# Two transformer-like blocks on one core: the first block's branch products between the gate chunks

## The chip, the core and the metric

The kernel runs on one core of a Trainium2 chip. Its engines are PE (matrix products), DVE (elementwise on vectors), ACT (activations and casts), POOL and SP, which issues most of the loads. Time is the device time of one execution in microseconds (us); the median of several executions is compared.

## What is computed

A sequence of 256 positions with 1024 channels goes through a first block and then twice through a second one. The change touches the first part of the first block, which in the reference is

```
u = rms_norm(h, norm_mix_pre)
proj = u @ w_in            # 10 slots of 256 columns, then 4 x 1024 gate columns
y_a = rg_lru_branch(a_x, a_gate, ...)        # linear recurrence   (branch 0)
y_b = pool_branch(p_x, ...)                  # window means        (branch 1)
y_c = hgrn2_branch(c_q, c_f, c_i, c_g, ...)  # chunked recurrence  (branch 2)
y_d = short_conv_branch(s_b, s_c, s_x, ...)  # 3-tap convolution   (branch 3)
merged = sum over k of sigmoid(gate_logits[k]) * (y[k] @ w_branch[k])
h = h + rms_norm(merged @ w_out, norm_mix_post)
```

## The kernel before, in words

Channels lie on partitions and the 256 positions on the free axis. Every weight is used in float32 precision by splitting it: a chunk of 128x2048 words is loaded by SP into `raw` (2 buffers), ACT casts it to `hi` (L190, 3 buffers) and DVE subtracts to get `lo` (L192, 3 buffers). A chunk then feeds 48 matmuls (L230), three for each pair of a weight tile and an input tile: hi x H, hi x L and lo x H, where H and L are the split input. `weights` takes chunks from a queue that `plan1` writes down in order of use, and calls for two chunks beyond the one it hands out.

A result of a chunk goes to a PSUM tile `mm` of 128x512. PSUM is parted by the pools of `Builder`: three tiles for `mm`, one for sums, three for the small products of the branches, one for later use.

The order of the first block's program is: the ten slot chunks (`win` 0 to 9), then the branches `hgrn`, `short_conv`, `pool`, `lru`, then sixteen gate chunks, four each for the branches 3, 1, 0, 2 (`BORDER`), then the four branch products in the same order, then `wout` (`post`). A gate chunk's result is multiplied by the norm (L946, DVE) and put through a sigmoid (L947, ACT). A branch product uses one `wbr` chunk for four PSUM tiles of 12 matmuls; each tile is multiplied by its gate (L958, DVE) and, from the second branch on, added to the merged result M (L961, DVE). With the last branch M is split into H and L in permuted order (L346 on ACT, L347 on DVE), which are the input `xs` of `wout`.

`lru` is the linear recurrence. On DVE it has a convolution (L1069 to L1073), two reciprocals of 128x512 (L1088, L1091), a chain of multiplications (L1092 to L1097), two scans (L1100) and the last product (L1108), which `finish` splits.

Nothing of the order on an engine is written by hand. Engines take their instructions in an order that is fixed when the program is built: where several could start next on an engine, by the builder's own estimate of times, the one that stands first in the program is taken; an instruction from further on is put in where those before it must still wait. Each engine then follows its own list strictly, and waits where an operand is late.

Of the kernel before, what the change touches and what calls it, by code (L numbers as in the profile page):

```python
# [17 lines left out]
P = 128  # L18
NT = 256
# [738 lines left out]

WINDOWS = (2, 4, 8, 16)
MLEV = (1, 2, 4, 8, 16)  # L760
BORDER = (3, 1, 0, 2)


def layout1(A):
# [24 lines left out]
    m = [s == t]  # L789
    for h in MLEV:  # L790
        m.append((s // (2 * h) == t // (2 * h)) & (s % (2 * h) < h) & (t % (2 * h) >= h))
# [10 lines left out]

class Block1(Builder):
    def plan1(self):
        for j in SLOTS + [10 + 4 * k + j for k in BORDER for j in range(4)]:
            self.plan("win", j)
        for k in BORDER:
            self.plan("wbr", k)
        self.plan_pairs("wout", 4, KD)
        self.plan_pairs("wup", 16, KD)  # L810
        self.plan_pairs("wdown", 4, DFF // P)
# [59 lines left out]
    def block1(self):  # L871
        nc = self.nc
        v = nc.vector

        X = self.X
        XS = [self.slot(8 + j, [P, 2, NT]) for j in range(4)]
        self.X = XS
        norm = self.Norm(self, "norm_mix_pre")

        def first(j):  # L880
            nc.sync.dma_start(XS[j], self.d["xs"][:, 2 * j:2 * j + 2])
            norm.feed(j, False)

        self.ahead = 0
        self.weights("win", SLOTS[0], first=first)
        nc.scalar.dma_start(self.ident, self.d["ident"])
        H, L = norm.H, norm.L
        pt0 = self.mm("win", SLOTS[0], KD, H, L)
        norm.sums()
        norm.done()  # L890
        self.X = X
        nc.sync.dma_start(self.prmt[:, self.n1:], self.d["prm"][:, self.n1:])
        bd = self.slot(16, [P, 6, P])
        nc.sync.dma_start(bd.rearrange("p a b -> p (a b)"), self.d["bd"])
        lm = self.slot(7, [P, 6, P], I32)
        nc.sync.dma_start(lm.rearrange("p a b -> p (a b)"), self.d["lmask"])
        s6 = self.slot(6, [P, 4, NT])
        winv = self.half(s6, 0)
        nc.sync.dma_start(winv, self.d["winv"].rearrange("p (a b) -> p a b", a=2))
        bones = self.tp.tile([P, 2], F32, name="bones", tag="bones", bufs=1)  # L900
        nc.sync.dma_start(bones, self.d["bones"])
        for j in range(4):
            nc.sync.dma_start(X[j], self.d["xp"][:, 2 * j:2 * j + 2])

        sp = self.softplus_neg(self.prm("lru_lambda"))
        c4 = self.tp.tile([P, 2], F32, name="c4", tag="c4", bufs=1)
        v.tensor_scalar(c4, sp, 4.0, None, op0=ALU.mult)
        hb = self.tp.tile([P, 4], F32, name="hba", tag="hba", bufs=1)
        v.tensor_scalar(hb[:, :2], self.prm("lru_b_a"), 0.5, None, op0=ALU.mult)
        v.tensor_scalar(hb[:, 2:], self.prm("lru_b_x"), 0.5, None, op0=ALU.mult)  # L910
        lb = self.tp.tile([P, 2, 4], F32, name="lb", tag="lbt", bufs=1)
        d = self.prm("hgrn_lower_bound")
        v.tensor_sub(lb[:, :, 0], d, d)
        nc.scalar.activation(lb[:, :, 0], lb[:, :, 0], AF.Exp)
        v.reciprocal(lb[:, :, 1], lb[:, :, 0])
        v.tensor_mul(lb[:, :, 0], lb[:, :, 0], lb[:, :, 1])
        v.tensor_sub(lb[:, :, 2], lb[:, :, 0], lb[:, :, 0])
        v.tensor_scalar(lb[:, :, 3], lb[:, :, 2], -1.0, 1.0, op0=ALU.mult, op1=ALU.add)

        S = [self.slot(i, [P, 4, NT]) for i in range(6)]  # L920
        dest = {0: self.half(S[0], 0), 1: self.half(S[0], 1), 3: self.half(S[2], 0),
                4: self.half(S[2], 1), 5: self.half(S[3], 0), 6: self.half(S[3], 1), 7: self.half(S[4], 0),
                8: self.half(S[4], 1), 9: self.half(S[5], 0)}
        pad = self.slot(1, [P, 2, 16 + NT])
        nc.gpsimd.memset(pad[:, :, :16], 0.0)
        dest[2] = pad[:, :, 16:]
        for j in SLOTS:
            pt = pt0 if j == SLOTS[0] else self.mm("win", j, KD, H, L)
            v.tensor_mul(dest[j], pt, norm.rb2)
        YS = {}  # L930
        self.hgrn(dest, lb, lm, bones, YS)
        self.short_conv(dest, YS)
        self.pool(pad, winv, bd, YS)
        self.lru(dest, bd, c4, hb, S, s6, YS)
        gates = {}
        for n, k in enumerate(BORDER):
            for j in range(4):
                i = n * 4 + j
                if i % 2 == 0:
                    gs = self.slot(8 + i // 2, [P, 4, NT])  # L940
                gates[k, j] = self.half(gs, i % 2)
        M = [gates[BORDER[0], j] for j in range(4)]
        for k, j in gates:
            pt = self.mm("win", 10 + 4 * k + j, KD, H, L)
            g = gates[k, j]
            v.tensor_mul(g, pt, norm.rb2)  # L946
            nc.scalar.activation(g, g, AF.Sigmoid)  # L947
        for k in BORDER:
            h, lo = self.weights("wbr", k)
            YH, YL = YS[k]  # L950
            if k == BORDER[3]:
                MH, ML = self.new_xs()
            for j in range(4):
                pt = self.p_mm.tile([P, 2, NT], F32, name="mm")
                c = slice(j * 512, (j + 1) * 512)
                self.mm_pair(pt, h[:, c], lo[:, c], YH, YL, range(2), True, True)
                g = gates[k, j]
                v.tensor_mul(g, pt, g)  # L958
                if k == BORDER[0]:
                    continue  # L960
                v.tensor_add(M[j], M[j], g)  # L961
                if k == BORDER[3]:
                    for i in range(2):
                        self.split(M[j][:, i].rearrange("p (i a c) -> p c a i", i=16, a=4, c=4),
                                   MH[2 * j + i].rearrange("p (c a i) -> p c a i", c=4, a=4, i=16),
                                   ML[2 * j + i].rearrange("p (c a i) -> p c a i", c=4, a=4, i=16))
        nx = self.Norm(self, "norm_mlp_pre")
        self.post("wout", KD, MH, ML, "norm_mix_post", nx)
        hid = [self.slot(j, [P, 4, NT], F32R) for j in range(16)]
        HH = [hid[k // 2][:, k % 2] for k in range(32)]  # L970
        HL = [hid[k // 2][:, 2 + k % 2] for k in range(32)]
        for j, pt in self.mms("wup", 16, nx.H, nx.L, True):
            if j == 0:
                nx.done(True)
            z = self.t2("z")
            v.tensor_mul(z, pt, nx.rb2)
            f = self.t2("f")
            v.scalar_tensor_tensor(f, z, 0.0, z, op0=ALU.max, op1=ALU.mult)
            self.split(f, hid[j][:, :2], hid[j][:, 2:])
        norm = self.Norm(self, "ffn1_norm0")  # L980
        self.post("wdown", 32, HH, HL, "norm_mlp_post", norm)
        return norm
# [128 lines left out]
    def hgrn(self, dest, lb, lm, bones, YS):  # L1111
# [25 lines left out]
        def products(qs, ks, lev):  # L1137
            ps = [bank() for _ in range(2)]
            for b in range(2):
                bs = slice(b * P, (b + 1) * P)  # L1140
                for i in range(2):
                    for e in range(2):
                        nc.tensor.matmul(ps[e][:, b, i], ks[rows[e], i, bs], qs[rows[e], i, bs], start=True, stop=True)
            for e in range(2):
                v.copy_predicated(sc[e].rearrange("p a b c -> p (a b) c"),
                                  lm[:, lev][:, None, :].to_broadcast([P, 4, P]),
                                  ps[e].rearrange("p a b c -> p (a b) c"))
# [4 lines left out]
        while h <= 128:  # L1152
            qh, kh = self.t2("qh"), self.t2("kh")
            view = lambda t: flat(t).rearrange("p (n two h) -> p n two h", two=2, h=h)
            if h <= 16:
                v.tensor_mul(qh, q, pre)
                v.tensor_mul(kh, k, suf)
                products(qh, kh, 1 + MLEV.index(h))
            else:
# [59 lines left out]
SLOTS = [4, 3, 5, 6, 7, 8, 9, 2, 0, 1]  # L1219
# [44 lines left out]
```

## Time and profile before

| | us |
|---|---|
| median of 3 runs | 1833.76 |
| lowest and highest of them | 1829.9, 1835.49 |
| the profiled execution | 1830.46 |
| its span in the trace | 1828.4 |

The page gives each engine's busy time as a share of the span; times in all views count from the span's start. The block that the change touches takes roughly the first 320 us; the moved code lies between 75 and 222 us.

### The profile page before, as it was taken

To read this page: it belongs to the slowest core of one execution; us is meant where nothing else is said; L and a number is where in the kernel's file an instruction comes from. 1 tells how busy PE (TensorE), PEld (TensorE's weight loads), DVE (VectorE), ACT (ScalarE), POOL (GpSimd) and SP (SyncE) were. 2 spreads that over 40 slices of the span, in tenths; PEclk is the share of its full clock that TensorE was granted. 3 is DMA by queue.
4 is the path that set the end of the run, shared out by engine and by line. 5 is a ranking of instruction groups with operands and counts; after the bars stand their busy time and mean duration, and the time that the engine had idled before them with its cause. 6 is when DMAs were issued, how large, how long until landed. Compare 5 with 4: busy or idle time off the path is not lost.

```text
span 1828.4 us, 32906 instructions
## 1 busy us (share of the span) xinstructions
PE 1764.5 (97%) x14048; PEld 1688.6 (92%) x14048; DVE 1325.3 (72%) x2021; ACT 922.0 (50%) x1047; POOL 46.0 (3%) x69
## 2 busy tenths in 40 slices
PE   7999999999999999989999999999998989999998
PEld 7989899999999987778999999999997778999997
DVE  7886877546765698988876656765598988776653
ACT  5354454435444455467654445444455566654442
POOL 0000000000100000000000000100000000000000
PEclk9999999999999999999999999999999999999999
DMA  7526445554555579886455555555569887355552
GB/s 267 184 93 209 163 160 185 185 185 161 194 185 180 190 220 260 267 227 160 150 187 193 186 170 199 191 188 176 194 202 279 251 234 180 126 198 185 185 185 93
DMA packets 53569, 348.46 MB, mean 191 GB/s; under 512 B 6192, under 2 KB 6320, under 8 KB 14256
## 3 DMA queue, kind: packets, MB, share of 16 engines
q1 hardware_dynamic: 47376, 308.66, 47.4%
q0 software_dynamic: 4896, 35.65, 10.5%
q8 instruction: 110, 1.80, 0.4%
q10 hardware_dynamic: 1152, 2.06, 0.3%
q14 instruction: 35, 0.29, 0.0%
HBM read 345.30 MB, written 1.05 MB: 189 GB/s over the span
## 4 chain that ended last, share of the span: by engine, by line
PE 73%; DMA 10%; DVE 7%; ACT 6%; issue 3%; ACTq 0%; DVEq 0%
PE mm L230 65%; DMA raw<-qkv 7%; ACT hi L190 3%; DVE lo L192 3%; DMA raw<-gat 2%; PE mm L253 1%; PE y L605 1%; PE tr L597 1%; PE pc L312 1%; PE pc L322 1%; ACT lo L188 1%; PE sc L580 1%; DMA raw<-out 1%; PE sc L584 0%; ACT zsq L538 0%
## 5 line engine op out<-in xcount | busy, mean ns | idle before, releaser
L230 PE MATMUL mm<-xs,hi 128*128 128x256 f32 x5440 | 966.9, 281 | 8.2 <-ACT hi L181 5.8
L230 PEld LDWEIGHTS mm<-xs,hi 128*128 128x128 f32 x5440 | 827.1, 189 | 15.6 <-ACT hi L181 5.8
L192 DVE TENSOR_TENSOR lo<-raw,hi 128x2048 fp32r<-128x2048 f32 (+1 forms) x254 | 573.3, 2257 | 314.2 <-ACT hi L190 313.3
L190 ACT CAST hi<-raw 128x2048 fp32r<-128x2048 f32 (+1 forms) x288 | 541.9, 1884 | 424.5 <-PE mm L230 354.8
L230 PE MATMUL mm<-xs,lo 128*128 128x256 f32 x2720 | 736.9, 281 | 8.4 <-DVE lo L192 4.1
L230 PEld LDWEIGHTS mm<-xs,lo 128*128 128x128 f32 x2720 | 502.1, 189 | 12.6 <-DVE lo L192 4.9
L230 PE MATMUL mm<-slot,hi 128*128 128x256 f32 x2304 | 399.8, 278 | 3.2 <-DVE slot L958 2.4
L230 PEld LDWEIGHTS mm<-slot,hi 128*128 128x128 f32 x2304 | 345.3, 188 | 4.2 <-DVE slot L958 2.8
L230 PE MATMUL mm<-slot,lo 128*128 128x256 f32 x1152 | 306.0, 278 | 0.0
L230 PEld LDWEIGHTS mm<-slot,lo 128*128 128x128 f32 x1152 | 209.8, 188 | 0.0
L642 DVE SCALAR_TENSOR_TENSOR slot<-slot,prm,slot 128x256 f32<-128x256 f32 x360 | 149.2, 480 | 0.0
L346 ACT CAST slot<-f 128x256 fp32r<-128x256 f32 (+1 forms) x104 | 45.3, 438 | 194.2 <-DVE f L434 191.9
L522 PE MATMUL mm<-lo,xs 128*128 128x512 f32 x288 | 116.0, 403 | 17.2 <-DMA lo<-qkv 17.0
L523 PE MATMUL mm<-hi,xs 128*128 128x512 f32 x288 | 113.9, 396 | 0.0
L521 PE MATMUL mm<-hi,xs 128*128 128x512 f32 x288 | 113.3, 393 | 0.0
L188 ACT ACTIVATE lo<-raw 128x2048 fp32r<-128x2048 f32 x34 | 65.1, 1915 | 81.1 <-DMA raw<-qkv 57.1
L522 PEld LDWEIGHTS mm<-lo,xs 128*128 128x128 f32 x288 | 54.4, 189 | 34.6 <-DMA lo<-qkv 23.9
L347 DVE TENSOR_TENSOR slot<-f,slot 128x256 fp32r<-128x256 f32 (+1 forms) x104 | 48.9, 473 | 37.8 <-ACT slot L346 37.6
L428 DVE TENSOR_TENSOR z<-mm,rb 128x512 f32<-128x512 f32 x88 | 60.4, 690 | 8.2 <-ACT rb L340 1.3
L521 PEld LDWEIGHTS mm<-hi,xs 128*128 128x128 f32 x288 | 54.5, 189 | 11.5
L523 PEld LDWEIGHTS mm<-hi,xs 128*128 128x128 f32 x288 | 54.6, 189 | 10.6
L642 DVE SCALAR_TENSOR_TENSOR spare<-slot,prm,spare 128x256 f32<-128x256 f32 x120 | 49.9, 474 | 0.0
(277 smaller groups left out, 1295.5 us busy)
## 6 DMA issues: line engine op xcount, KB each, us to landing
raw<-ffn1u SPq DMA_DIRECT2D x44, 1024.0 KB, 4.8
raw<-ffn2u SPq DMA_DIRECT2D x44, 1024.0 KB, 4.8
raw<-qkv SPq DMA_DIRECT2D x36, 1024.0 KB, 7.0
raw<-win SPq DMA_DIRECT2D x24, 1024.0 KB, 4.9
lo<-qkv POOLq DMA_DIRECT2D x18, 1024.0 KB, 9.0
raw<-wup SPq DMA_DIRECT2D x16, 1024.0 KB, 4.8
raw<-wdown SPq DMA_DIRECT2D x16, 1024.0 KB, 4.8
raw<-ffn1d SPq DMA_DIRECT2D x16, 1024.0 KB, 4.9
```

The source lines that it names most:

```text
L188: nc.scalar.mul(lo[:, :w], r[:, :w], -1.0)
L190: nc.scalar.copy(h[:, :w], r[:, :w])
L192: nc.vector.tensor_sub(lo[:, :w], r[:, :w], h[:, :w].bitcast(F32))
L230: nc.tensor.matmul(pt[:, m], w[:, i, c], x[k], start=first and m == 0 and i == 0 and j == 0, stop=last and i == n - 1 and j == 2, skip_gro ...
L253: nc.tensor.matmul(pts[e][:, m], wt[:, k, m * P:(m + 1) * P], (H, L)[x][k], start=k == 0 and w == x == m == 0, stop=k == KD - 1 and w == 1 ...
L346: nc.scalar.copy(H, src)
L347: return nc.vector.tensor_sub(L, src, H.bitcast(F32))
L428: nc.vector.tensor_mul(z, pt, norm.rb2)
L521: nc.tensor.matmul(pz[j], H[k][:, js], h[:, w], start=k == 0, stop=False)
L522: nc.tensor.matmul(pz[j], H[k][:, js], lo[:, w], start=False, stop=False)
L523: nc.tensor.matmul(pz[j], L[k][:, js], h[:, w], start=False, stop=k == 7)
L642: nc.vector.scalar_tensor_tensor(acc[i], u, w, acc[i], op0=ALU.mult, op1=ALU.add)
```

## The change

The branch products are no longer a loop behind all gates. The product of a branch stands in the program behind the first gate chunk of the next branch; the last one stands behind all gates. `lru` stands behind the second gate chunk instead of ahead of the first. The queue of chunks is written in the same new order. Tiles for two gate chunks are taken as they are needed, and not all ahead of the gates.

```diff
+LRU = 1
...
     def plan1(self):
-        for j in SLOTS + [10 + 4 * k + j for k in BORDER for j in range(4)]:
+        for j in SLOTS:
             self.plan("win", j)
-        for k in BORDER:
-            self.plan("wbr", k)
+        for n, k in enumerate(BORDER):
+            for j in range(4):
+                self.plan("win", 10 + 4 * k + j)
+                if n and j == 0:
+                    self.plan("wbr", BORDER[n - 1])
+        self.plan("wbr", BORDER[3])
...
         self.pool(pad, winv, bd, YS)
-        self.lru(dest, bd, c4, hb, S, s6, YS)
         gates = {}
...
-        for k, j in gates:
+        def gate(n, k, j):
...
             pt = self.mm("win", 10 + 4 * k + j, KD, H, L)
             g = gates[k, j]
             v.tensor_mul(g, pt, norm.rb2)
             nc.scalar.activation(g, g, AF.Sigmoid)
-        for k in BORDER:
+
+        def branch(k, last=False):
             h, lo = self.weights("wbr", k)
             YH, YL = YS[k]
-            if k == BORDER[3]:
-                MH, ML = self.new_xs()
             for j in range(4):
                 pt = self.p_mm.tile([P, 2, NT], F32, name="mm")
...
                 v.tensor_add(M[j], M[j], g)
-                if k == BORDER[3]:
+                if last:
...
+        M = None
+        for n, k in enumerate(BORDER):
+            for j in range(4):
+                gate(n, k, j)
+                if n == 0 and j == LRU:
+                    self.lru(dest, bd, c4, hb, S, s6, YS)
+                if n and j == 0:
+                    M = M or [gates[BORDER[0], i] for i in range(4)]
+                    branch(BORDER[n - 1])
+        MH, ML = self.new_xs()
+        branch(BORDER[3], True)
```

## Rows read from the trace of the kernel before

**Rows 1.** The page, part 1 and its head: busy us, share of span, instructions.

```profile
span 1828.4 us, 32906 instructions
PE 1764.5 (97%) x14048; PEld 1688.6 (92%) x14048; DVE 1325.3 (72%) x2021; ACT 922.0 (50%) x1047; POOL 46.0 (3%) x69
```

**Rows 2.** Busy time by stretches: start:end, length, engines, granted clock, DMA share, GB/s.

```profile
117.00:145.00 28.00, 25.20 (x214) 24.79 (x213) 25.49 (x27) 18.33 (x24) 0.00 (x0) 1.00 0.28 97
145.00:187.50 42.50, 42.50 (x367) 42.50 (x366) 23.96 (x16) 19.03 (x16) 0.00 (x0) 1.00 0.61 210
187.50:213.50 26.00, 23.42 (x195) 22.64 (x193) 24.17 (x29) 8.78 (x7) 0.00 (x0) 1.00 0.52 175
213.50:222.00 8.50, 7.57 (x59) 7.18 (x60) 8.32 (x13) 5.79 (x10) 0.00 (x0) 1.00 0.19 82
```

**Rows 3.** Whom PE waited for in 75 to 222 us: total, times, longest.

```profile
PE mm L230 <- DVE lo L192: 2.8, 2, 2.5
PE mm L230 <- DVE slot L958: 2.4, 2, 1.3
...
PE mm L230 <- ACT xs L346: 0.8, 2, 0.6
...
PE mm L230 <- DVE xs L347: 0.2, 1, 0.2
```

**Rows 4.** DVE's instructions in order, 117 to 145: start, us, idle time before.

```profile
117.28 0.68 DVE L946 TENSOR_TENSOR slot<-mm,rb 128x512 f32<-128x512 f32 x1
...
120.53 3.35 DVE L1088 RECIPROCAL slot<-slot 128x512 f32<-128x512 f32 x1
...
128.22 0.68 DVE L1092 TENSOR_TENSOR slot<-slot,slot 128x512 f32<-128x512 f32 x1
128.81 2.29 DVE L192 TENSOR_TENSOR lo<-raw,hi 128x2048 fp32r<-128x2048 f32 x1
...
132.82 0.69 DVE L946 TENSOR_TENSOR slot<-mm,rb 128x512 f32<-128x512 f32 x1
...
134.96 2.28 DVE L192 TENSOR_TENSOR lo<-raw,hi 128x2048 fp32r<-128x2048 f32 x1
137.16 1.27 DVE L1100 TENSOR_TENSOR_SCAN slot<-slot 128x256 f32<-128x256 f32 x2
138.34 0.67 DVE L946 TENSOR_TENSOR slot<-mm,rb 128x512 f32<-128x512 f32 x1
138.93 0.68 DVE L1108 SCALAR_TENSOR_TENSOR slot<-gsq,slot 128x512 f32<-128x512 f32 x1
139.53 2.28 DVE L192 TENSOR_TENSOR lo<-raw,hi 128x2048 fp32r<-128x2048 f32 x1
...
142.33 1.33 DVE L946 TENSOR_TENSOR slot<-mm,rb 128x512 f32<-128x512 f32 x2
```

**Rows 5.** PE's instructions in order, where gate chunks 4, 5 and 6 meet.

```profile
122.40 0.63 PE L230 MATMUL mm<-xs,hi 128*128 128x256 f32 x4
...
128.00 0.63 PE L230 MATMUL mm<-xs,hi 128*128 128x256 f32 x4
131.16 0.38 PE L230 MATMUL mm<-xs,lo 128*128 128x256 f32 x1 [2.53 <-DVE lo L192]
```

**Rows 6.** DVE's instructions in order, in the branch products and their end.

```profile
198.18 1.28 DVE L958 TENSOR_TENSOR slot<-mm,slot 128x512 f32<-128x512 f32 x2
199.38 1.28 DVE L961 TENSOR_TENSOR slot<-slot,slot 128x512 f32<-128x512 f32 x2
...
218.32 2.26 DVE L347 TENSOR_TENSOR xs<-slot,xs 128x256 fp32r<-128x256 f32 x4
```

**Rows 7.** Busy time by stretches of 2 us, as rows 2: the granted clock.

```profile
32.00:34.00 2.00, 1.16 (x16) 0.97 (x16) 2.00 (x2) 1.56 (x1) 0.00 (x0) 1.00 0.01 5
34.00:36.00 2.00, 1.67 (x8) 1.67 (x9) 2.00 (x4) 0.00 (x0) 0.00 (x0) 0.61 0.22 37
36.00:38.00 2.00, 2.00 (x12) 2.00 (x12) 2.00 (x2) 0.00 (x0) 0.00 (x0) 0.54 0.95 393
...
244.00:246.00 2.00, 1.91 (x9) 1.91 (x10) 2.00 (x5) 1.10 (x4) 0.00 (x0) 0.50 0.00 0
246.00:248.00 2.00, 2.00 (x11) 2.00 (x11) 2.00 (x5) 1.36 (x4) 0.00 (x0) 0.50 0.00 0
```

**Rows 8.** DVE finishing the short convolution; the `wbr` loads, issue to landing.

```profile
101.86 0.68 DVE L347 TENSOR_TENSOR slot<-yd,slot 128x512 fp32r<-128x512 f32 x1
...
DMA to landing us min/median/max: 4.7/5.5/6.1
```

More of the change, by code (lines that the diff above doesn't have):

```diff
@@ L933, in block1 @@
         self.pool(pad, winv, bd, YS)
-        self.lru(dest, bd, c4, hb, S, s6, YS)
         gates = {}
[L936 to L942, printed above, removed]
-        for k, j in gates:
+        def gate(n, k, j):
+            i = n * 4 + j
+            if i % 2 == 0:
+                gates[k, j + 1] = self.slot(8 + i // 2, [P, 4, NT])
+            gates[k, j] = self.half(gates[k, j + 1], 0) if i % 2 == 0 else self.half(gates[k, j], 1)
             pt = self.mm("win", 10 + 4 * k + j, KD, H, L)
```

## The prediction, made before the changed kernel ran

> **What bounds the kernel now.** I read the page first: PE is busy 97% of the span, DVE 72% [rows 1]. So a microsecond is won only where PE waits, and a change of order alone can win no more than the waits of its own stage. The second view was busy time by stretches around the code that is moved [rows 2]. The reader is to see stretch length minus PE busy: 2.80 us lost in 117 to 145 (the linear recurrence on DVE), nothing in 145 to 187.5 (gate chunks alone), 2.58 in 187.5 to 213.5 (branch products), 0.93 in 213.5 to 222 (their end and the first `wout` chunk). 6.3 us in all, 0.34% of the span. About 0.3% (5.5 us) is what a measurement of this kernel can tell from no change, so a gain that counts needs nearly all of them.
>
> The third view, who PE waited for [rows 3], gives the cause: 2.8 us for `lo` of a weight chunk, 2.4 for the products' multiplication L958 to empty a PSUM tile, 1.0 for `xs` of the merged result. DVE is behind each; it is busy 25.5 of 28 us in the first stretch and 24.2 of 26 in the third [rows 2].
>
> The fourth view is the order of DVE's instructions in the recurrence [rows 4], and of PE's chunks beside it [rows 5]. A gate chunk takes PE 5.60 us (122.40 to 128.00, the same place of two chunks [rows 5]). Counting the multiplications L946 from 85.9 us, that at 117.28 is of gate chunk 3, that at 132.82 of chunk 4, that at 138.34 of chunk 5 [rows 4]. So chunk 4 ends on PE at about 122.65 (two matmuls of the next chunk are in the row at 122.40), but its PSUM tile is emptied only by 133.5: **the multiplication comes 10 us late.** The recurrence stands ahead of the gates in the program and takes DVE whenever its next instruction is ready. Something later in the program comes in only where an instruction must await the one just before it: behind L1092 (`lo` of chunk 6), behind L1094 (the multiplication of chunk 4), behind L1096 (`lo` of chunk 7), behind the scan (the multiplication of chunk 5), behind L1108 (`lo` of chunk 8) [rows 4]. Of two that wait, the earlier in the program goes first. Today the lateness is nearly free, since a gate chunk uses one of three PSUM tiles per 5.6 us.
>
> **The change, part by part.** Matmuls, casts, DVE operations and bytes are the same in number; everything is a matter of place.
>
> *The recurrence behind two gate chunks.* It now yields to gate chunks 0 and 1 and to the weights of chunks 2 and 3. Chunk 3's multiplication is at 117.28 and the recurrence's first long DVE instruction at 120.53 [rows 4], so nothing it yields to is still to be done. I cost this at 0; if HGRN were faster and the recurrence earlier, it would move by a chunk, 5.6 us, inside the same stretch.
>
> *Four loads of `wbr` moved in SP's queue.* Same bytes, other order; landing takes 4.7 to 6.1 us [rows 8] and the DMA share around is 0.28 to 0.61 [rows 2]. Two raw buffers keep loads ahead of a 5.6 us chunk. The `win` loads now behind them come one chunk later, as their use does. 0; without this cover a load would show at most its 6.1 us once.
>
> *The branch stage, emptied.* A branch with additions costs DVE four multiplications (0.60 apart), four additions (0.60) and a `lo` (2.28), 7.1 us against PE's 5.6, so today DVE falls behind from branch to branch [rows 6]. Four gate chunks stand between two branches in the new order, each 0.69 + 2.28 = 3.0 us of DVE per 5.6 us, so the debt is paid there. Of the 3.5 us lost in 187.5 to 222 [rows 2], only the end remains: the last branch still has its splits. Its DVE work is 2.4 + 2.4 + 8 x 0.56 (L347 [rows 6]) + 2.28 = 11.6 us from its first finished tile (1.4 us in), so done about 13 us in; PE wants the last two slices about 4.2 us into `wout`, 9.8 us in, but has half of the next `wout` chunk (2.8 us) to put between. I leave 1.0 us there (bounds 0 and 2.2). **Gain 2.5 us** (bounds 1.3 and 3.5).
>
> *The first branch product inside the recurrence.* Its inputs are ready (short convolution finished at 101.86 [rows 8]), so it goes on PE right behind gate chunk 4, at 122.65, as four tiles of 1.4 us. With three PSUM tiles, tile 0 takes that of gate chunk 2, tile 1 that of chunk 3 (emptied at 118), tile 2 that of chunk 4, tile 3 that of tile 0, and gate chunk 5 that of tile 1. Tiles 0 and 1 end at 125.45. Nothing ahead of chunk 4's multiplication on DVE has changed, so it still ends at 133.5: **PE waits 8.05 us**. Tile 2 runs to 134.9. At the next opening, behind L1096, `lo` (now of chunk 6, whose weights are called for before the product's tiles) still goes first; tile 0's multiplication takes the opening behind the scan and ends at 139.0: **PE waits 4.1 us more**. Tile 1's comes behind L1108, by 140.2, as tile 3 ends at 140.4. Gate chunk 5 starts there, not at 122.65 + 5.6 = 128.25. The wait is 12.15 us, where the same stretch loses 2.80 now (its `lo`, done at 131, is then early): **loss 9.35 us**. Behind PE's wait the whole chain of gates and branches queues, and no later stage has idle time to take it up (145 to 187.5 has none [rows 2]).
>
> Nothing shows this wait yet, so its bounds are wide: below, no wait at all and the 2.80 gone; above, all these multiplications only where DVE is free again, at 142.33 [rows 4], which puts tile 2 at 142.9 and chunk 5 at 145.7, 17.45 us lost, 14.65 more than now. I take the opening-by-opening value, since L946 at 132.82 and 138.34 sits in just those openings.
>
> *The clock behind the wait.* After a thin stretch PE's granted clock is 0.61 and 0.54 in 34 to 38, which costs 0.8 + 0.9 = 1.7 us, and 0.50 in 244 to 248 [rows 7], the lower of its levels (1.2 of 2.4 GHz). After the 2.5 us wait at 128.6 [rows 5] it stayed 1.00 in its stretch [rows 2]. A wait of 8 us is nearer to the former: **loss 1.7 us** (bounds 0 and 3.4, twice that row).
>
> On this the Trainium skill reads otherwise: "TensorE: Matmul & The Clock Gate", section "Loop structure matters more than you think", says that a DVE copy out of PSUM does not break the engine's warmth, while a long wait for a DMA does. By it this term would be 0 and the sum 1.7 us lower. The trace has a wait on DVE of 2.5 us that agrees, and none on DVE alone as long as 8 us.
>
> **Sum:** -2.5 + 9.35 + 1.7 = +8.55 us on the profiled execution of 1830.46 (span 1828.4 and 2.1 around it), 1839.0. That execution lies 3.3 us under the median of the runs shown, 1833.76; against the median I forecast 1842. Bounds: -3.5 - 2.8 = -6.3 to -1.3 + 14.65 + 3.4 = +16.8, 1827.5 to 1850.5.
>
> **Rivals** (each against the median of 1833.76).
> *One opening better.* Tile 0's multiplication goes ahead of a `lo` that is late, or chunk 4's takes the first opening (128.8). Against: a `lo` wins at 128.81 and 134.96 [rows 4]. For: the first-branch weights shift the casts by a chunk. Chunk 4's emptied at 129.5 gives PE waits of 4.05 and, with tile 0 next behind L1094 at 133.5, 2.6, 6.65 in all: +3.85 - 2.5 and perhaps the clock, +1.4 to +3.1. 1836.
> *The other side: the recurrence no longer holds the gates up.* If chunk 4's multiplication comes when PE is done, at about 123, the product flows. It decides for a gain once tile 2 waits under 3 us. The stretch's 2.8 and the branch stage's 2.5 go: -5.3, 1828.5; with the end wholly covered -6.3, 1827.5. For: the recurrence yields to more than before. Against: what it yields to is past by 117.28 [rows 4].
> *Everything late.* All multiplications behind the recurrence: +14.65 + 1.7 - 2.5, +13.9, 1847.5.
> *It does nothing:* PE merely trades 2 or 3 us of wait between the two places, 1834.
>
> **How the numbers follow.** Forecast 0.54, one opening better 0.20, the other side 0.13, everything late 0.07, nothing 0.06. The forecast's own range is 1838 to 1847. Slower by over 0.3% begins at 1839.3: most of the first (0.48), everything late (0.07), a little of the second (0.02): 0.57. Faster begins at 1828.3: under half of the other side, 0.06. The rest, 0.37, lies between. Range 1830 to 1848: it holds the first two, the last and half of "late", leaving out most of the other side.
>
> **What would show it.** In the new trace: L946 of gate chunk 4 between L1094 and L1095, PE waiting there for it with the products' tiles on both sides (8 us), then for L958 behind the scan (4 us); a granted clock well under 1 after it; no wait for L958 between later gate chunks, and about 1 us at `wout`. I am wrong if chunk 4's multiplication stands at about 123 us, if the first product runs elsewhere than behind chunk 4, or if PE fills the wait with other work.

## The result, and the profile after

| | kernel before | changed kernel |
|---|---|---|
| median of 9 runs, us | 1831.20 | 1841.72 |
| lowest and highest | 1826.96, 1835.49 | 1837.45, 1849.66 |
| ratio to before, 95% interval | | 1.0057 [1.0038, 1.0076] |
| profiled execution | 1830.46 | 1849.66 |
| first matmul of `wup` (L253) in it | 244.1 | 252.1 |

The change makes the kernel slower by some 0.57%, 10 us, with an interval of 7 to 14. The profiled execution is the slowest of the nine, 19 us above that of before, so its end says little; the moved code's own stretch is read up to the first matmul of `wup`, the next thing that both kernels do alike, and that comes 8.0 us later. The two executions do not reach the moved code at the same time, though. Up to the first gate multiplication DVE's instructions are the same in both; it stands here in the kernel before, and here in the changed one:

```profile
85.93 0.68 DVE L946 TENSOR_TENSOR slot<-mm,rb 128x512 f32<-128x512 f32 x1
```

```profile
85.18 0.68 DVE L948 TENSOR_TENSOR slot<-mm,rb 128x512 f32<-128x512 f32 x1
```

Counted from that multiplication, `wup` comes after 158.2 and 166.9 us: the change costs 8.7 us in these two executions.

The changed kernel's page, part 1 and its head:

```profile
span 1847.9 us, 32908 instructions
PE 1775.7 (96%) x14048; PEld 1699.7 (92%) x14048; DVE 1325.9 (72%) x2021; ACT 923.1 (50%) x1047; POOL 46.1 (2%) x69
```

The work is the same in number as in [rows 1]. Busy time by stretches, the first four as in [rows 2], and the 8 us behind them:

```profile
117.00:145.00 28.00, 17.45 (x123) 16.95 (x122) 24.44 (x26) 14.05 (x18) 0.00 (x0) 0.82 0.21 75
145.00:187.50 42.50, 42.42 (x364) 42.25 (x363) 25.60 (x22) 17.27 (x14) 0.00 (x0) 1.00 0.51 178
187.50:213.50 26.00, 25.92 (x223) 25.75 (x222) 18.02 (x16) 10.93 (x9) 0.00 (x0) 1.00 0.56 196
213.50:222.00 8.50, 8.18 (x68) 7.78 (x68) 6.36 (x9) 4.47 (x5) 0.00 (x0) 1.00 0.57 180
...
222.00:230.00 8.00, 7.53 (x60) 7.01 (x59) 7.89 (x12) 4.72 (x8) 0.00 (x0) 1.00 0.18 74
```

Length minus PE busy: 10.55 us are lost in the stretch of the recurrence, where it was 2.80, and 0.08 + 0.08 + 0.32 + 0.47 = 0.95 from there to the end of the products, where it was 3.51 [rows 2]. Whom PE waited for, 75 to 240 us, against [rows 3]:

```profile
PE mm L230 <- DVE slot L948: 8.0, 1, 8.0
PE mm L230 <- DVE slot L959: 2.8, 2, 2.6
...
PE mm L230 <- ACT xs L346: 0.3, 1, 0.3
PE mm L230 <- DVE xs L347: 0.2, 1, 0.2
```

L948 is the gate's multiplication (L946 before), L959 the product's (L958 before). DVE's instructions in order, against [rows 4]; the recurrence's lines stand 13 further down in the changed file:

```profile
116.56 0.68 DVE L948 TENSOR_TENSOR slot<-mm,rb 128x512 f32<-128x512 f32 x1
...
127.50 0.68 DVE L1105 TENSOR_TENSOR slot<-slot,slot 128x512 f32<-128x512 f32 x1
128.10 2.28 DVE L192 TENSOR_TENSOR lo<-raw,hi 128x2048 fp32r<-128x2048 f32 x1
...
131.51 0.69 DVE L1107 TENSOR_TENSOR slot<-slot 128x512 f32<-128x512 f32 x1
132.11 0.68 DVE L948 TENSOR_TENSOR slot<-mm,rb 128x512 f32<-128x512 f32 x1
...
134.25 2.28 DVE L192 TENSOR_TENSOR lo<-raw,hi 128x2048 fp32r<-128x2048 f32 x1
136.45 1.27 DVE L1113 TENSOR_TENSOR_SCAN slot<-slot 128x256 f32<-128x256 f32 x2
137.63 0.67 DVE L959 TENSOR_TENSOR slot<-mm,slot 128x512 f32<-128x512 f32 x1
138.21 0.68 DVE L1121 SCALAR_TENSOR_TENSOR slot<-gsq,slot 128x512 f32<-128x512 f32 x1
138.81 1.28 DVE L959 TENSOR_TENSOR slot<-mm,slot 128x512 f32<-128x512 f32 x2
```

Every opening is filled as forecast: `lo`, chunk 4's multiplication, `lo`, tile 0's multiplication behind the scan, tile 1's behind the last product (tile 2's, ready by then, directly follows it). PE's instructions in order, where the two waits end:

```profile
132.85 0.80 PE L230 MATMUL mm<-slot,hi 128*128 128x256 f32 x2 [7.97 <-DVE slot L948]
...
135.15 0.63 PE L230 MATMUL mm<-slot,hi 128*128 128x256 f32 x2
138.35 0.51 PE L230 MATMUL mm<-slot,hi 128*128 128x256 f32 x2 [2.58 <-DVE slot L959]
```

Both interrupted matmuls belong to the product (`slot` input): its third tile waits 7.97 us, its fourth 2.58. Busy time by stretches of 2 us, for the clock:

```profile
131.00:133.00 2.00, 0.15 (x1) 0.15 (x1) 2.00 (x4) 0.17 (x1) 0.00 (x0) 0.50 0.78 233
133.00:135.00 2.00, 2.00 (x10) 2.00 (x11) 2.00 (x4) 0.46 (x1) 0.00 (x0) 0.50 0.72 299
135.00:137.00 2.00, 0.78 (x4) 0.48 (x3) 2.00 (x2) 0.00 (x0) 0.00 (x0) 0.75 0.00 0
...
139.00:141.00 2.00, 2.00 (x13) 2.00 (x12) 2.00 (x4) 1.15 (x2) 0.00 (x0) 0.60 0.84 356
141.00:143.00 2.00, 2.00 (x12) 2.00 (x11) 0.90 (x2) 1.36 (x1) 0.00 (x0) 0.55 0.00 0
```

### The profile page after: what moved, and what is told of

Read it like the earlier page. It is cut to its first block, busy times and chain, and to the rows that moved or that the text cites. A ratio compares the mean times of both kernels' runs of the same rounds, so it can differ in the third digit from the quotient of the medians.

```text
span 1847.9 us, 32908 instructions
## 1 busy us (share of the span) xinstructions
PE 1775.7 (96%) x14048; PEld 1699.7 (92%) x14048; DVE 1325.9 (72%) x2021; ACT 923.1 (50%) x1047; POOL 46.1 (2%) x69
## 4 chain that ended last, share of the span: by engine, by line
PE 72%; issue 8%; DMA 8%; DVE 6%; ACT 5%; POOL 0%; SPq 0%; DVEq 0%; ACTq 0%; POOLq 0%
PE mm L230 64%; DMA raw<-qkv 4%; ACT hi L190 3%; DVE lo L192 2%; DMA raw<-gat 2%; PE mm L253 1%; PE y L605 1%; PE tr L597 1%; PE pc L312 1%; PE pc L322 1%; PE sc L580 1%; DMA raw<-out 1%; DMA lo<-qkv 0%; DVE slot L642 0%; DMA raw<-win 0%
```

## The experiments

All ratios are to the kernel before, with 95% intervals; "`wup` at" is the first matmul of `wup` in the profiled execution (before 244.1, changed 252.1). DVE's list is the same in all these kernels up to the first gate multiplication, but that comes anywhere from 83.60 to 86.90 in their profiled executions; so "`wup` at" alone can mislead by up to 3 us, and where that matters the time is counted from that multiplication (before 158.2, changed 166.9).

**The recurrence's place undone.** `recurrence_ahead` puts the recurrence back ahead of the gates and leaves the products where the change has them.

```diff
         self.pool(pad, winv, bd, YS)
+        self.lru(dest, bd, c4, hb, S, s6, YS)
         gates = {}
...
-                if n == 0 and j == LRU:
-                    self.lru(dest, bd, c4, hb, S, s6, YS)
```

> The changed kernel with the recurrence back ahead of all gates in the program. What it yields to is done before it starts, so the order of every engine's work should be the changed kernel's: ratio 1.0055 within its interval, 7 to 9 us up to the first matmul of wup. If the recurrence's place matters, that differs by 2 us or more.

Measured: 1.0039 [1.0027, 1.0051], `wup` at 251.3, waits of 8.0 us for the gate's multiplication and 2.8 for the products'. In the two traces DVE, ACT and POOL run the same instructions in the same order from start to end, and PE does past 800 us. So the recurrence's move does nothing, and this is a second measurement of the changed kernel, whose interval overlaps the first. Its span is 1833.7 us with the same stage: behind the first matmul of `wup` it takes 1582.4 us, the first profiled execution of the changed kernel 1595.8, that of before 1584.3. The 11.5 us by which the first profile exceeds the stage's loss come and go between executions: the profiled execution of `recurrence_behind`, below, the slowest of its twelve, has 1594.8 behind `wup` too.

**One part alone.** `first_product_alone` moves one product; three stay behind all gates.

```diff
+PRODUCT = {(1, 0): 3}
+REST = (1, 0, 2)
...
-                if n and j == 0:
+                if (n, j) in PRODUCT:
                     M = M or [gates[BORDER[0], i] for i in range(4)]
-                    branch(BORDER[n - 1])
+                    branch(PRODUCT[n, j])
...
-        branch(BORDER[3], True)
+        for k in REST:
+            branch(k, k == BORDER[3])
```

> The kernel before with one part of the change: the first product behind gate chunk 4 (the recurrence behind gate chunk 1, as changed); the other three products behind all gates, as before. Theory A: the whole loss is this product's, so the waits for L948 and L959 stay at 8.0 and 2.6 us, the clock drops behind them, and nothing is won later: 10 to 11 us up to the first matmul of wup, ratio 1.0055 to 1.007. Were the loss a sum over all interleaved products, a third of it: 1.002.

Measured: 1.0044 [1.0028, 1.0061], `wup` at 253.0, 8.9 us late, where 10 to 11 were forecast. But this execution reaches the first gate multiplication at 83.60, the earliest of all; counted from it, the loss is 11.2 us, 2.5 more than the changed kernel's. Whom PE waited for, 75 to 240 us:

```profile
PE mm L230 <- DVE slot L951: 8.0, 1, 8.0
PE mm L230 <- DVE slot L962: 5.0, 3, 2.6
```

The first wait is whole, and the second row has 2.6 us beside the recurrence plus 2.4 of the old waits of the branch stage. The one product carries the loss; the other three, spread, are the gain. The ratio is under the forecast, though its interval reaches into it.

**Other PSUM tiles, same order.** `psum_apart` takes three of the first product's tiles from the PSUM pool of the branches' small products.

```diff
             for j in range(4):
-                pt = self.p_mm.tile([P, 2, NT], F32, name="mm")
+                if k == BORDER[0] and j < 3:
+                    pt = self.p_sc.tile([P, 2, NT], F32, name="pf", tag="sc")
+                else:
+                    pt = self.p_mm.tile([P, 2, NT], F32, name="mm")
```

> The changed kernel, in which three of the first branch product's four tiles come from the PSUM pool of the small products; the order of every engine's work stays. Theory A (PE waits because the product's third and fourth tile need PSUM tiles whose multiplications are placed late among the recurrence's): the waits for L948 (8.0 us) and behind it (2.6) are gone, PE runs to the next gate chunk and waits there some 3 us for its lo, the clock stays at 1.00, and the ratio to the kernel before is about 0.9985. Theory B (DVE has more work in this stretch than PE, whatever the tiles): about the same 10 us are lost at another wait, ratio about 1.006.

Measured: 0.9992 [0.9982, 1.0002], `wup` at 242.8. Busy time in the recurrence's stretch, and whom PE waited for:

```profile
117.00:145.00 28.00, 24.10 (x202) 23.49 (x202) 25.85 (x29) 16.86 (x22) 0.00 (x0) 1.00 0.21 75
```

```profile
PE mm L230 <- DVE lo L192: 3.9, 3, 2.5
...
PE mm L230 <- DVE slot L962: 0.2, 1, 0.2
```

No wait for a multiplication above 0.2 us is left, the clock stays at 1.00, and the stretch loses 3.90 us, to `lo`, where some 3 were forecast. DVE's work did not change, and its order is the changed kernel's up to 142 us, past the end of both waits (behind that some instructions change places). So the 10 us were a wait for tiles and no lack of DVE time.

**The recurrence behind the first product.** `recurrence_behind` keeps tiles and work, and changes what goes first.

```diff
-                if n == 0 and j == LRU:
-                    self.lru(dest, bd, c4, hb, S, s6, YS)
                 if n and j == 0:
                     M = M or [gates[BORDER[0], i] for i in range(4)]
                     branch(BORDER[n - 1])
+                    if n == 1:
+                        self.lru(dest, bd, c4, hb, S, s6, YS)
```

> The changed kernel with the recurrence put behind the first branch product in the program, so that gate chunk 4, the first product and the weights called for by then go first on DVE; same work, same PSUM tiles. Theory A: chunk 4's multiplication comes within 1 us of its end, no wait for L948 or L959 above 1 us, the wait for lo mostly gone too; 4 to 5.5 us under the kernel before, ratio 0.997 to 0.998. Theory B (too much DVE work): the loss stays, ratio above 1.003. A third, that interleaving itself costs (more changes between gates and products, other loads): ratio above 1.002 with no single wait to show for it.

Measured: 0.9973 [0.9960, 0.9987], `wup` at 240.1. The recurrence's old stretch, and whom PE waited for:

```profile
117.00:145.00 28.00, 28.00 (x235) 27.79 (x234) 24.55 (x22) 18.80 (x23) 0.00 (x0) 1.00 0.40 135
```

```profile
PE mm L230 <- ACT hi L190: 2.0, 1, 2.0
```

PE is never idle from 117 to 145. Chunk 4 ends on PE at about 120.7, and its multiplication now comes at once:

```profile
121.22 0.68 DVE L948 TENSOR_TENSOR slot<-mm,rb 128x512 f32<-128x512 f32 x1
```

Three PSUM tiles are enough, and DVE has the same work, part of it now behind 145: it is the order on DVE that costs. One wait of 2.0 us appears at the new end of the recurrence, where gate chunk 9 follows the second product. The view puts it down to a cast. ACT's, DVE's and PE's instructions there:

```profile
156.23 1.90 ACT L190 CAST hi<-raw 128x2048 fp32r<-128x2048 f32 x1 [2.12 <-PE mm L230]
```

```profile
157.37 1.28 DVE L959 TENSOR_TENSOR slot<-mm,slot 128x512 f32<-128x512 f32 x2
```

```profile
158.19 0.47 PE L230 MATMUL mm<-xs,hi 128*128 128x256 f32 x2 [2.05 <-ACT hi L190]
```

The cast ends at 158.13, but the first of the two multiplications, that of the second product's tile 1, whose place chunk 9 needs, ends 0.1 us before it. `behind_and_apart`, below, shows which of the two PE waited for.

**The products clear of the recurrence.** `products_later` has `PRODUCT = {(2, 0): 3, (2, 2): 1, (3, 0): 0}`, in the form above, and the recurrence as changed.

> The changed kernel with the first product behind gate chunk 8 and the second behind chunk 10, past the recurrence; the third and fourth where they are. Theory A: the stretch of the recurrence is as in the kernel before (2.8 us lost to lo), the branch stage keeps its gain of 2.5 to 2.9 us, ratio about 0.9985. If interleaving itself costs: above 1.002.

Measured: 1.0000 [0.9989, 1.0011], `wup` at 245.1. The big waits are gone, but so is the forecast gain. Whom PE waited for, 117 to 200 us, and the clock behind the first of the two:

```profile
PE mm L230 <- DVE lo L192: 2.5, 1, 2.5
PE mm L230 <- DVE slot L960: 1.4, 1, 1.4
```

```profile
131.00:134.00 3.00, 2.34 (x14) 2.35 (x15) 3.00 (x6) 0.00 (x0) 0.00 (x0) 0.74 0.50 112
134.00:137.00 3.00, 3.00 (x20) 3.00 (x20) 3.00 (x5) 1.06 (x2) 0.00 (x0) 0.69 0.56 238
```

A product's tile waits 1.4 us for its multiplication, and the clock fell behind the wait for `lo`, which costs at most 0.26 x 3 + 0.31 x 3 = 1.7 us. In this execution the two are large enough to take up the 2.6 us. The fall of the clock does not belong to this order, however: in `order_before_apart`, which has DVE's list of the kernel before, it fell too behind the same wait (0.76, 0.50 and 0.89 in 131 to 137). What took up the gain in the eleven other executions is not shown.

**A shorter recurrence.** `short_recurrence` leaves out the two reciprocals of the changed kernel's recurrence.

```diff
-        v.reciprocal(rec, rec)
+        v.tensor_scalar(rec, rec, 1.0, None, op0=ALU.mult)
...
-        v.reciprocal(rs, rs)
+        v.tensor_scalar(rs, rs, 1.0, None, op0=ALU.mult)
```

> The changed kernel, which leaves out the recurrence's two reciprocals of 128x512 (each 3.35 us on DVE): a multiplication by 1.0 (0.4 us) stands in the place of each. Theory A (the recurrence on DVE holds the multiplications up): chunk 4's multiplication comes within 2 us of its end, the waits for L948 and L959 fall from 10.6 us to under 3, ratio 0.997 to 1.000. Theory C (three PSUM tiles are too few for four product tiles beside gate chunks, whatever DVE does): over 5 us of wait stay.

Measured: 1.0024 [1.0011, 1.0038], `wup` at 250.1. Theory A's number fell: 8.0 us of wait remain, 7.8 of them in one place. DVE's instructions in order, and PE's where it resumes:

```profile
124.35 0.68 DVE L948 TENSOR_TENSOR slot<-mm,rb 128x512 f32<-128x512 f32 x1
...
126.75 0.68 DVE L959 TENSOR_TENSOR slot<-mm,slot 128x512 f32<-128x512 f32 x1
127.35 0.68 DVE L1107 TENSOR_TENSOR slot<-slot 128x512 f32<-128x512 f32 x1
129.23 2.29 DVE L192 TENSOR_TENSOR lo<-raw,hi 128x2048 fp32r<-128x2048 f32 x1 [1.20 <-ACT hi L190]
...
136.37 0.66 DVE L959 TENSOR_TENSOR slot<-mm,slot 128x512 f32<-128x512 f32 x1
```

```profile
137.18 0.77 PE L230 MATMUL mm<-xs,hi 128*128 128x256 f32 x2 [7.78 <-DVE slot L959]
```

Chunk 4's multiplication does come at once (124.35), and tile 0's too. But tile 1, computed by about 126.7, is multiplied at 136.37, and gate chunk 5 needs its place. Meanwhile DVE stands idle for 1.20 us for a cast whose `lo` its list has next. The multiplication stands in the list behind two `lo` and most of the rest of the recurrence. Theory C's number fits this run, but three tiles are enough in `recurrence_behind`. What fits both runs: a list fixed at build time keeps a ready multiplication behind earlier work, here even after that work was cut by some 6 us.

**A second step.** `behind_and_later` adds to `recurrence_behind` the second product two chunks later, `PRODUCT = {(1, 0): 3, (2, 2): 1, (3, 0): 0}`.

> The kernel with the recurrence behind the first product, and the second product two gate chunks later, behind chunk 10, clear of the recurrence's end. If the 2.0 us that PE waits there for hi come from the second product's work joining the recurrence's on DVE, they go: 5 to 6 us under the kernel before, ratio 0.9967. If they come from loads that the recurrence made late, they stay: ratio 0.9973.

`behind_and_apart` instead takes three tiles of every product from the free pool (`if j < 3`).

> The kernel with the recurrence behind the first product, and three tiles of each product from the PUSM pool of the small products. No wait for L962 is left; if PSUM tiles still cost something beside the recurrence's end, 1 to 2 us more are won, ratio 0.9965; if only late loads do, nothing changes: 0.9973.

Measured: 0.9967 [0.9952, 0.9982] with `wup` at 238.2, and 0.9956 [0.9939, 0.9972] with `wup` at 236.9. In both the 2.0 us are gone, so late loads were not the cause. In `behind_and_apart` the second product keeps its place and its work, and the cast named above comes at the same time; PE's and ACT's instructions there:

```profile
155.84 0.40 PE L230 MATMUL mm<-xs,hi 128*128 128x256 f32 x2
```

```profile
156.08 1.91 ACT L190 CAST hi<-raw 128x2048 fp32r<-128x2048 f32 x1 [2.14 <-PE mm L230]
```

Chunk 9 starts here before that cast does, so it never needed it: in `recurrence_behind` PE waited for the PSUM tile, whose multiplication came late behind the recurrence's last instructions. It is the main wait once more, only smaller, under another engine's name. The intervals of 0.9973, 0.9967 and 0.9956 overlap; that each step gains is seen in the traces, where `wup` comes 154.4, 152.5 and 151.4 us behind the first gate multiplication. Tiles apart also shorten the end of the last product: 16.48 of 16.50 us busy in 213.5 to 230. All three together, `all_three`:

> The recurrence behind the first product, the second product behind chunk 10, three tiles of each product apart. If the two measures save the same wait, ratio as behind_and_apart, 0.9956; if they add up, 0.9945.

Measured: 0.9959 [0.9945, 0.9973], `wup` at 237.9, 151.4 us behind the first gate multiplication, as in `behind_and_apart`. In the traces the two save the same wait and do not add up; the ratio's interval alone, which reaches 0.9945, could not tell.

**The order of before, tiles apart.** `order_before_apart` gives the kernel before the three tiles and nothing else.

> The kernel before, with its order of work, in which three tiles of each branch product come from the PSUM pool of the small products. If the branch stage's waits for L958 (2.4 us) are waits for a tile, they go, and some of the end's with them: 2 to 3 us, ratio 0.9985. If DVE's debt of work sets that stage, the wait only moves to the first matmuls of wout: 1.000.

Measured: 0.9996 [0.9983, 1.0009], `wup` at 246.5. Whom PE waited for, 75 to 240 us:

```profile
PE mm L230 <- ACT xs L346: 3.3, 1, 3.3
PE mm L230 <- DVE lo L192: 2.5, 1, 2.5
```

The waits for L958 are gone and return as one of 3.3 us at `wout`, behind which the clock fell (0.50 in 214 to 218, 0.65 in 218 to 222). In the branch stage it is DVE's debt that counts: other tiles alone do not pay it, spreading the products does.

## Why the prediction was right

The forecast was 1842, measured 1841.72; slower, with the mechanism as described. That the two agree to 0.3 us is luck: the forecast put 8.55 us on a median of 1833.76 of three runs, and the change measured is 10.5 us on one of 1831.20 of nine. Part by part:

- *The recurrence's place, 0.* Right: the lists are the same without it, and `recurrence_ahead` measures the same within the intervals.
- *The branch stage, a gain of 2.5 us.* The trace has 0.95 us left of 3.51, a gain of 2.6. `order_before_apart` shows that other tiles alone do not win it.
- *The first wait, 8.05 us.* Measured 7.97, and in the opening that was named.
- *The second wait, 4.1 us.* Measured 2.58. The wait ends where forecast, behind the multiplication after the scan, but tile 2 ran at the lower clock and took from 132.85 to 135.78, 2.9 us and not 1.4. So the slow clock ate 1.5 us of a wait that was there anyhow; the sum of waits was put 1.5 us too high and the clock in that place cost nothing.
- *The clock, 1.7 us.* In 139 to 143 it is 0.60 and 0.55, 0.8 + 0.9 = 1.7 us, as the row at 34 to 38 us had it [rows 7]. The fall is shown, its size to a tenth is luck: in `recurrence_ahead`, with the same lists, the same stretches cost 1.0 + 0.1 = 1.1 us.

```profile
139.00:141.00 2.00, 2.00 (x11) 2.00 (x11) 1.69 (x3) 0.60 (x1) 0.00 (x0) 0.50 0.79 332
141.00:143.00 2.00, 2.00 (x18) 2.00 (x17) 0.69 (x1) 1.69 (x1) 0.00 (x0) 0.94 0.00 0
```

By the prediction's reading of the Trainium skill, "TensorE: Matmul & The Clock Gate", section "Loop structure matters more than you think", this term would have been 0. That reading went too far: in the sketch there the next matmuls follow the DVE copy immediately, and here PE stood waiting 7.97 us for DVE. The trace shows 0.50 behind that wait.

- *The sum, +8.55.* Counted from the first gate multiplication up to `wup` the trace has +8.7 (+8.0 from the span's start). Its parts: 10.55 - 2.80 = 7.75 more of waits, 1.5 for tile 2 at the slow clock, 1.7 of clock at 139 to 143, less 2.6 of gain, make +8.35; 0.4 is not accounted for. The two measurements of this program, 1.0057 and 1.0039, are +10 and +7 us and lie on either side.

Of the rivals, "the other side" is refuted as a description of this change, and `recurrence_behind` makes it true: there chunk 4's multiplication is early, and 0.27% is won, of the 0.34% that PE lost in these stretches. "Everything late" and "one opening better" did not occur. Left open is what part of the 3 us between the two measurements of the changed kernel is chance; no row read here behind `wup` ties it to the change.

## What to carry to other kernels

When work with several short PSUM tiles is moved next to a long chain on the engine that empties them, count how many instructions of that chain stand ahead of each emptying in the engine's fixed list; busy shares don't show it, and a shorter chain did not cure it (10.6 us of wait became 8.0). Put the chain later in the program when its result is not wanted soon: here that turned a loss of 0.4 to 0.6% into a gain of 0.3%; with tiles from another pool 0.44% was measured, in an interval that overlaps. Two measures can save the same wait, and one part of a change can lose more than the others win: measure each part alone before judging the change. And when a view names who ended a wait, look whether another operand came at almost the same moment.

## What the runs showed of the hardware

PE's clock fell to 0.50 behind a wait of 7.97 us for DVE. A shorter one is not safe either: behind the 2.53 us wait for `lo` it stayed at 1.00 in the kernel before and in `psum_apart`, and fell to 0.74 and 0.69 in `products_later`; in `order_before_apart`, with DVE's list of the kernel before, it fell to 0.50 behind 2.52 us. So this differs between executions and not only between orders. And a low clock that falls into another wait cost nothing here: the 2.9 us of the third tile shortened the wait behind it by as much as they exceeded 1.4.
